# Expert weights in 2 MB loads and 16 KB slots, and the down bias inside one pair

## The chip, the core and the metric

The kernel runs on one core of a Trainium2 chip. The metric is the device time of one execution in microseconds (us). "MB" is 1024 KB where it counts a load, and a rate in GB/s is as the profile gives it.

## What is computed

A batch of one with 256 tokens, 16 meta tokens put ahead of them, width 1024, one layer, all in float32: a layer norm, a mixer with two branches (attention with forget gates, and an S5 state space scan), a residual norm, and a mixture of 32 experts of which each token uses four.

```python
h = layer_norm(concat(meta, x), ln_in_g, ln_in_b)                  # 272 x 1024
proj = h @ w_in                                                    # q, k, v, f, u, gates a and b
y_a = forgetting_attention(q, k, v, log_sigmoid(f + b_f))
y_b = gelu(s5_ssm(u, a_re, a_im, log_dt, b, c, d)); y_b = y_b * sigmoid(y_b @ w_glu + b_glu)
mix = (sigmoid(g_a) * (y_a @ w_up_a) + sigmoid(g_b) * (y_b @ w_up_b)) @ w_o
h = layer_norm(ALPHA * h + mix, ln1_g, ln1_b)
top_v, top_i = top_k(h @ w_router + b_router, 4); comb = softmax weights scattered to 32 columns
for e in range(32):
    gate = minimum(h @ w_gate[e] + b_gate[e], 7)
    up = clip(h @ w_up[e] + b_up[e], -7, 7)
    out += comb[:, e:e + 1] * (((up + 1) * gate * sigmoid(1.702 * gate)) @ w_down[e] + b_down[e])
return layer_norm(ALPHA * h + out, ln2_g, ln2_b)[:, 16:]
```

## The kernel before

**The front** (0 to about 283 us) is everything up to the router. Weights of the projections come in slabs (`slab`, L104) of 2 MB, each as two loads of 1 MB into two 8 KB slots of pool `wA`. `wA` has six slots, so three slabs stand at a time; the next waits until TensorE (PE) has used an old one. Small operands come between them: the router weights `wr` (L567) and its bias `brow` (L568) are loaded after the third slab that `w_in` gives behind the small loads. GpSimd (POOL) multiplies `wr` by the columns of the layer norm (`wrg`, L675 and L677), and VectorE (DVE) reduces that to `wsum` (L676, L678), which is used only much later, by the router. On the same two engines run the S5 preparation: sine and cosine by powers on DVE (`sn`, `cs`, `ew`), then `lr` (L358), the complex coefficients, the powers `E`, the matrices `bb`, and on POOL `cL`, `q` and `bz`. DVE then starts the forget gate (`fx`, `fa`, L535 and L536), ScalarE (ACT) finishes it (L537) and empties the projection tiles `kA`, `qA` from PSUM (L550 to L556), then `bT` (L462), which PE needs for the scan's `pb` (L481). PE runs the projections (`ps`, L214) and the transposes of `bz` (L461) between them. The order on each engine in the front is set by a scheduler, from the order of the code and its own estimates; each engine then runs its instructions strictly in that order.

**The experts** run in pairs, 15 pairs and then two single ones. PE and SP follow the order of the code here. Each expert has three matrices of 4 MB. `gate_up` (L1062) computes gate and up for 64 rows of gathered tokens, `act_T` transposes, `down` (L1094) does the down product of both experts of a pair, `combine` (L1124) adds the pair's result to `acc`. A matrix comes in quarters: 256 rows, two rows to a partition, 1 MB, with 8 KB in one piece per partition (`expert_load`, L728). Eight matmuls use one quarter in `gate_up`.

All of these loads are issued by SP on one queue, in the order in which PE uses them. Each waits for its slot to be free and for the load eight places before it, since completions go around eight counters (`DMAHW0` to `DMAHW7`). Slots are given in a fixed rota (`homes`): five of `wC`, seven of `wB`, six of `wA`, and the storage of `gate1` and `hT`, 20 slots, to which the storage of `acc` is added once, so 21 MB stand in SBUF before PE starts the experts. The last quarter of all is loaded as two halves (L711).

The rows of the down bias `b_down` (32 x 1024) are loaded in pair 5 into a slot of the rota (L717) and multiplied by the routing weights in pairs 8 and 9 (`down_bias`).

Of the kernel before, what the change touches and what calls it, by code (L numbers as in the profile page):

```python
# [20 lines left out]
P = 128  # L21
D = 1024
# [11 lines left out]
NWA, NWB, NWC = 6, 7, 5  # L34
# [14 lines left out]
def hybrid_trunk_kernel(ctx: ExitStack, tc: tile.TileContext, x, meta, ln_in_g, ln_in_b, w_in, b_f,  # L49
# [44 lines left out]
    prowP = sp.tile([8, 256], F32, name="prowP")  # L94
    ldt = sp.tile([16, 2], F32, name="ldt")

    def slab(src, kt):

        n = src.shape[1]
        src = src.rearrange("(k p) n -> p k n", p=P)  # L100
        nk, ks = 2048 // n, []
        for k0 in range(0, kt, nk):
            v_ = wA.tile([P, 2048], F32, name="w", tag="w").rearrange("p (k n) -> p k n", n=n)
            nc.sync.dma_start(v_, src[:, k0:k0 + nk])  # L104
            ks += [v_[:, k] for k in range(nk)]
        return ks
# [21 lines left out]
    for j, a in enumerate((ln1_g, ln1_b)):  # L128
        nc.sync.dma_start(prowP[4 * j:4 * j + 4], a.rearrange("l (q n) -> (l q) n", n=256))
# [140 lines left out]
    for k in range(2):  # L270
        TE.transpose(pp[:, 8 * k:8 * k + 8], prowP[:, k::2], ident[:8, :8])
# [438 lines left out]
    def part_load(t_, w, e, qtr, k):  # L710
        nc.sync.dma_start(t_[:, k], w[0, e, 256 * qtr:256 * qtr + 256].rearrange("(p k) n -> k p n", k=2)[k])  # L711

    def load_rows(rows):
        pool, tag = home[nload[0]]
        nload[0] += 1
        t_ = pools[pool].tile([P, 2048], F32, name="w", tag=tag)[:rows.shape[0], :D]
        nc.sync.dma_start(t_, rows)  # L717
        return t_

    def expert_load(w, e, qtr, load=True):  # L720
        key = (w.tensor.name, e, qtr)
# [37 lines left out]
    prefetch(2)  # L759
# [39 lines left out]
    prefetch(NWB - 4)  # L799
# [250 lines left out]
    def gate_up(e, between=None):  # L1050
        c0 = CAP * (e % 2)
        pos_ = []
        for j, (w, tag) in enumerate(((w_gate, "pg"), (w_up, "pu"))):
            pt = pg.tile([P, 512], F32, name=tag, tag=tag)
            for qtr in range(4):
                if between and (j, qtr) == (1, 1):
                    between()
                wt = expert_load(w, e, qtr)
                for k in range(2):
                    kk = 2 * qtr + k  # L1060
                    for n in range(2):
                        TE.matmul(pt[64 * n:64 * n + 64], XT[:, kk, c0:c0 + CAP], wt[:, k, n * 512:n * 512 + 512],  # L1062
# [24 lines left out]
    def down(p, aTs):  # L1087
        Yp = [py_.tile([P, 512], F32, name="Yp", tag=f"Yp{n}") for n in range(2)]
        for qtr in range(4):
            wd = [expert_load(w_down, 2 * p + g, qtr) for g in range(2)]  # L1090
            for k, n in ((0, 0), (0, 1), (1, 0), (1, 1)):
                half, j = qtr // 2, 2 * (qtr % 2) + k
                for g in range(2):
                    TE.matmul(Yp[n][64 * g:64 * g + 64], aTs[g][:, j, half],  # L1094
                              wd[g][:, k, n * 512:n * 512 + 512],
                              start=qtr == 0 and k == 0, stop=qtr == 3 and k == 1, skip_group_check=True)
# [3 lines left out]
    def down_one(e, aT):  # L1100

        Y = py_.tile([P, 512], F32, name="Yp", tag=f"Yp{e % 2}")
        for qtr in range(4):
            wd = expert_load(w_down, e, qtr)
            for k in range(2):
                half, j = qtr // 2, 2 * (qtr % 2) + k
# [248 lines left out]
```

## Time and profile before

| | us |
|---|---|
| median of 3 runs | 1225.4 |
| lowest, highest | 1223.43, 1225.46 |
| the profiled execution | 1222.52 |
| its span | 1221.0 |
| PE busy, share of the span | 1124.1, 92% |
| DVE busy, share | 340.4, 28% |
| ACT busy, share | 177.3, 15% |
| POOL busy, share | 71.6, 6% |
| chain that ended last | DMA 53%, PE 38%, DVE 5% |

The busy share of PE counts what it does at whatever pace the data allow. The chain that ended last is followed back from the last instruction, at each step to what released it. A stretch of it on DMA is time in which a load was under way on whose end the next step hung.

### The profile page before, as it was taken

How to read it: one execution, taken by the hardware profiler on the slowest of the kernel's cores; microseconds unless marked ns; L12 is line 12 of the kernel's file. 1: busy time of each engine (PE TensorE's matmuls, PEld its weight loads, DVE VectorE, ACT ScalarE, POOL GpSimd, SP SyncE). 2: the span in 40 equal slices, each digit the busy share in tenths (PEclk: the TensorE clock that was granted, in tenths of full speed). 3: DMA queues.
4: the chain of work that ended last, by engine and by line, in shares of the span. 5: the costliest groups of instructions: out<-in, count | busy, mean ns of one | idle time of the engine just before them, and what ended most of it. 6: DMA issues, size and time to landing. Idle time of an engine off the chain costs nothing.

```text
span 1221.0 us, 13200 instructions
## 1 busy us (share of the span) xinstructions
PE 1124.1 (92%) x5398; PEld 588.9 (48%) x5399; DVE 340.4 (28%) x782; ACT 177.3 (15%) x387; POOL 71.6 (6%) x118
## 2 busy tenths in 40 slices
PE   4889999998999999999999999998999899998994
PEld 2777788754545444444434363535433343443331
DVE  3969420533221212112131312130212121202013
ACT  2357410311101011010101010101010111101000
POOL 3333200400000000000000000000000000000001
PEclk9999999998999999999999999999999999999998
DMA  7742289557999999999999999999999999999992
GB/s 150 187 105 69 104 211 357 221 208 301 413 422 420 423 420 421 422 420 407 421 422 422 421 422 421 421 421 419 422 420 422 421 421 421 421 421 420 422 421 104
DMA packets 75674, 433.60 MB, mean 355 GB/s; under 512 B 14218, under 2 KB 14570, under 8 KB 26586
## 3 DMA queue, kind: packets, MB, share of 16 engines
q1 hardware_dynamic: 75178, 432.19, 89.3%
q8 instruction: 44, 0.72, 0.2%
q10 hardware_dynamic: 432, 0.52, 0.1%
q14 instruction: 20, 0.16, 0.0%
HBM read 431.64 MB, written 1.05 MB: 354 GB/s over the span
## 4 chain that ended last, share of the span: by engine, by line
DMA 53%; PE 38%; DVE 5%; ACT 1%; issue 1%; POOL 1%; SPq 1%; POOLq 0%; ACTq 0%; DVEq 0%
DMA w<-in_w_up_dram 29%; DMA w<-in_w_down_dram 16%; PE ps L214 7%; PE pu L1062 6%; PE pg L1062 6%; PE Yp L1094 5%; DMA w<-in_w_gate_dram 5%; PE ps L764 2%; PE px L945 2%; DMA w<-in_b_down_dram 2%; PE Yp L1108 1%; PE ps L936 1%; PE po L936 1%; PE px L1124 1%; DMA prow<-in_ssm_a_im_dram 1%
## 5 line engine op out<-in xcount | busy, mean ns | idle before, releaser
L1062 PE MATMUL pu<-w,xy 128*64 128x512 f32 x1024 | 238.5, 595 | 13.5 <-DMA w<-in_w_up_dram 13.5
L1062 PE MATMUL pg<-w,xy 128*64 128x512 f32 x1024 | 236.9, 594 | 3.3 <-PEq L1153 2.1
L1094 PE MATMUL Yp<-w,aT 128*64 128x512 f32 x960 | 228.1, 611 | 0.0
L1094 PEld LDWEIGHTS Yp<-w,aT 128*64 128x64 f32 x960 | 101.5, 141 | 114.7 <-issue 99.1
L1062 PEld LDWEIGHTS pu<-w,xy 128*64 128x64 f32 x1024 | 81.4, 136 | 154.8 <-issue 108.9
L1062 PEld LDWEIGHTS pg<-w,xy 128*64 128x64 f32 x1024 | 86.6, 137 | 140.4 <-issue 134.0
L214 PE MATMUL ps<-hT,w 128*128 128x256 f32 (+1 forms) x512 | 119.3, 392 | 2.8 <-ACT pr L595 2.8
L214 PEld LDWEIGHTS ps<-hT,w 128*128 128x128 f32 x512 | 98.0, 194 | 19.7 <-ACT pr L595 3.1
L1072 DVE TENSOR_SCALAR pg<-pg 128x512 f32<-128x512 f32 x32 | 22.4, 699 | 232.7 <-PE pg L1065 232.7
L1073 ACT ACTIVATE ups<-pg 128x512 f32<-128x512 f32 x32 | 19.1, 597 | 415.3 <-DVE pg L1072 415.3
L1075 DVE TENSOR_SCALAR pu<-pu 128x512 f32<-128x512 f32 x32 | 22.4, 700 | 186.8 <-PE pu L1065 186.8
L1097 DVE COPY xy<-Yp 128x512 f32<-128x512 f32 x15 | 10.4, 692 | 223.3 <-PE Yp L1094 223.3
L1124 PE MATMUL px<-xy,selT 128*128 128x512 f32 x120 | 61.7, 636 | 4.7 <-DVE acc L1126 2.6
L945 PE MATMUL px<-sel,z 128*128 128x128 f32 x480 | 59.8, 283 | 0.6 <-DVE sel L950 0.6
L1313 POOL TENSOR_TENSOR acc<-acc,gb 128x512 f32<-128x512 f32 (+1 forms) x2 | 2.4, 1214 | 979.6 <-ACT acc L1311 979.6
L945 PEld LDWEIGHTS px<-sel,z 128*128 128x128 f32 x480 | 58.6, 196 | 0.8 <-ACT aT L1084 0.8
L1124 PEld LDWEIGHTS px<-xy,selT 128*128 128x128 f32 x120 | 20.4, 193 | 42.3 <-DVE acc L1126 19.2
L1126 DVE TENSOR_TENSOR acc<-acc,px 128x512 f32<-128x512 f32 x56 | 37.3, 683 | 12.3 <-PE px L1124 12.2
L1098 ACT COPY xy<-Yp 128x512 f32<-128x512 f32 x15 | 8.8, 586 | 218.3 <-PE Yp L1094 218.3
L1084 ACT COPY aT<-px 128x512 f32<-128x512 f32 x32 | 18.8, 586 | 133.6 <-PE px L1082 133.6
L885 DVE TENSOR_SCALAR xy<-px,pcolP 128x128 f32<-128x128 f32 x60 | 23.7, 410 | 45.4 <-ACT xy L887 43.4
L887 ACT ACTIVATE xy<-px,pcolP 128x128 f32<-128x128 f32 x60 | 25.8, 455 | 44.6 <-PE px L945 42.6
(399 smaller groups left out, 838.2 us busy)
## 6 DMA issues: line engine op xcount, KB each, us to landing
w<-in_w_gate_dram SPq DMA_DIRECT2D x128, 1024.0 KB
w<-in_w_up_dram SPq DMA_DIRECT2D x128, 1024.0 KB
w<-in_w_down_dram SPq DMA_DIRECT2D x127, 1024.0 KB
w<-in_w_in_dram SPq DMA_DIRECT2D x16, 1024.0 KB
w<-in_w_o_dram SPq DMA_DIRECT2D x4, 1024.0 KB
w<-in_w_up_a_dram SPq DMA_DIRECT2D x2, 1024.0 KB
w<-in_w_up_b_dram SPq DMA_DIRECT2D x2, 1024.0 KB
w<-in_w_glu_dram SPq DMA_DIRECT2D x1, 1024.0 KB
```

Source lines behind the costliest of these rows:

```text
L214: TE.matmul(pt, w[k][:, j * P:(j + 1) * P], hT[:, k, n0:n1], start=k == 0, stop=k == KD - 1)
L764: TE.matmul(pt, w[k][:, d * P:(d + 1) * P], y[:, k], start=k == 0, stop=k == 3)
L885: V.tensor_scalar(out_, in_, g_, b_, op0=ALU.mult, op1=ALU.add)
L887: S.activation(out_, in_, AF.Identity, scale=g_, bias=b_)
L936: TE.matmul(po[i][n], mT[:, k, i * P:(i + 1) * P], wo[k // 2][:, k % 2, n * 512:n * 512 + 512], start=False, stop=k == KD - 1, skip_group_ ...
L945: TE.matmul(pts[k // 4][:, (k % 4) * P:(k % 4 + 1) * P], z1[:, i, paired(k)], sel[:, i].rearrange("p e s -> p (e s)"), start=i == 0 and k ...
L1062: TE.matmul(pt[64 * n:64 * n + 64], XT[:, kk, c0:c0 + CAP], wt[:, k, n * 512:n * 512 + 512], start=kk == 0, stop=False, skip_group_check=True)
L1072: V.tensor_scalar_min(pgt, pgt, 7.0)
L1075: V.tensor_scalar(put, put, 7.0, -7.0, op0=ALU.min, op1=ALU.max)
L1094: TE.matmul(Yp[n][64 * g:64 * g + 64], aTs[g][:, j, half], wd[g][:, k, n * 512:n * 512 + 512], start=qtr == 0 and k == 0, stop=qtr == 3 an ...
L1124: TE.matmul(pt, selT[:, i * P:(i + 1) * P], Ysb[:, ns], start=True, stop=True)
L1126: V.tensor_add(acc[:, i, ns], acc[:, i, ns], pt)
```

## The change

An expert's matrix comes in halves: 512 rows, four rows to a partition, 2 MB, with 16 KB in one piece per partition. The slots are 16 KB: four of `wA`, three of `wB`, two of `wC`. The storage of `gate1` and `hT` serves as one place of the rota together, as two loads of 1 MB; in the first round `acc` and `gate1` serve so. That makes ten places, 20 MB. The last half of all also comes as two loads of 1 MB. Which row of an expert's input stands on which partition (`paired`, the columns of the layer norm `pcolP`) follows the new layout. A slab of the front takes one `wA` slot of 16 KB, still with two loads of 1 MB, and four slabs stand at a time. `w_o` takes two slots instead of four. Load and use of `b_down` are both in pair 8. What the two kernels do when an expert has more than 64 tokens (`crowded`) is rewritten for the new slots too; with these inputs that branch isn't taken, and the diff leaves it out.

```diff
--- before
+++ after
-NWA, NWB, NWC = 6, 7, 5
+NWA, NWB, NWC = 4, 3, 2
...
-    prowP = sp.tile([8, 256], F32, name="prowP")
+    prowP = sp.tile([P, 512], F32, name="prowP", tag="etmp")[:4]
...
     def slab(src, kt):
 
         n = src.shape[1]
         src = src.rearrange("(k p) n -> p k n", p=P)
-        nk, ks = 2048 // n, []
+        nk = 2048 // n
+        v_ = wA.tile([P, 4096], F32, name="w", tag="w").rearrange("p (k n) -> p k n", n=n)
         for k0 in range(0, kt, nk):
-            v_ = wA.tile([P, 2048], F32, name="w", tag="w").rearrange("p (k n) -> p k n", n=n)
-            nc.sync.dma_start(v_, src[:, k0:k0 + nk])
-            ks += [v_[:, k] for k in range(nk)]
-        return ks
+            nc.sync.dma_start(v_[:, k0:k0 + nk], src[:, k0:k0 + nk])
+        return [v_[:, k] for k in range(kt)]
...
-    slots = [("wC", "w")] * NWC + [("wB", "w")] * (NWB - 4) + [("wA", "w")] * NWA + [("keep", "gate1")]
-    slots += [("wB", "w")] * 4 + [("fk", "hT")]
-    first = slots[:NWC + NWB + NWA - 3] + [("keep", "acc")] + slots[NWC + NWB + NWA - 3:]
+    PAIR = (("keep", "gate1"), ("fk", "hT"))
+    slots = [(("wC", "w"),)] * NWC + [(("wB", "w"),)] * (NWB - 2) + [(("wA", "w"),)] * NWA + [PAIR]
+    slots += [(("wB", "w"),)] * 2
+    first = slots[:NWC + NWB + NWA - 2] + [(("keep", "acc"), ("keep", "gate1"))] + slots[-2:]
...
-        while len(out) <= 12 * NE:
-            out += [s_ for s_ in slots if s_ != ("keep", "gate1") or len(out) < 9 * NE - 24]
-        return out[:12 * NE + 1]
+        while len(out) <= 6 * NE:
+            out += [s_ for s_ in slots if s_ != PAIR or len(out) < 9 * NE // 2 - 12]
+        return out[:6 * NE + 1]
...
-    def part_load(t_, w, e, qtr, k):
-        nc.sync.dma_start(t_[:, k], w[0, e, 256 * qtr:256 * qtr + 256].rearrange("(p k) n -> k p n", k=2)[k])
+    def part_load(t_, w, e, hf_, k0, nk):
+        nc.sync.dma_start(t_, w[0, e, 512 * hf_:512 * hf_ + 512].rearrange("(p k) n -> p k n", k=4)[:, k0:k0 + nk])
...
-    def expert_load(w, e, qtr, load=True):
-        key = (w.tensor.name, e, qtr)
+    def expert_load(w, e, hf_, nk=4):
+
+        key = (w.tensor.name, e, hf_)
         if key in ready:
             return ready.pop(key)
-        pool, tag = home[nload[0]]
+        place = home[nload[0]]
         nload[0] += 1
-        t_ = pools[pool].tile([P, 2048], F32, name="w", tag=tag).rearrange("p (k n) -> p k n", n=D)
-        if load:
-            nc.sync.dma_start(t_, w[0, e, qtr * 256:qtr * 256 + 256].rearrange("(p k) n -> p k n", k=2))
-        return t_
+        ks = []
+        for pool, tag in place:
+            n = 4 // len(place)
+            t_ = pools[pool].tile([P, n * D], F32, name="w", tag=tag).rearrange("p (k n) -> p k n", n=D)
+            for k0 in range(0, n, nk):
+                part_load(t_[:, k0:k0 + min(n, nk)], w, e, hf_, len(ks) + k0, min(n, nk))
+            ks += [t_[:, k] for k in range(n)]
+        return ks
...
     def paired(k):
 
-        return slice(256 * (k // 2) + k % 2, 256 * (k // 2) + 256, 2)
+        return slice(512 * (k // 4) + k % 4, 512 * (k // 4) + 512, 4)
...
-            for qtr in range(4):
+            for hf_ in range(2):
...
-                wt = expert_load(w, e, qtr)
-                for k in range(2):
-                    kk = 2 * qtr + k
+                wt = expert_load(w, e, hf_)
+                for k in range(4):
+                    kk = 4 * hf_ + k
...
         upA = activate(0, *gate_up(2 * p))
-        if p == 5:
+        if p in (6, 7):
+            residual(p - 6)
+        elif p == 8:
             bdown = [load_rows(b_down[0])]
-        elif p in (6, 7):
-            residual(p - 6)
-        elif p in (8, 9):
-            down_bias(p - 8)
+            for i in range(2):
+                down_bias(i)
...
-    for qtr in range(3):
-        ready[w_down.tensor.name, e + 1, qtr] = expert_load(w_down, e + 1, qtr)
-    last = expert_load(w_down, e + 1, 3, load=False)
-    for k in range(2):
-        part_load(last, w_down, e + 1, 3, k)
-    ready[w_down.tensor.name, e + 1, 3] = last
+    for hf_ in range(2):
+        ready[w_down.tensor.name, e + 1, hf_] = expert_load(w_down, e + 1, hf_, 4 - 2 * hf_)
```

On SP, in the front, from the first slab behind the small loads: before, `w_125` to `w_131` are two slabs, `w_613` and `w_615` the third.

```order
L104 DMA w_125<-in_w_in_dram 128x4x512 [waits DMAHW1_49]
L104 DMA w_127<-in_w_in_dram 128x4x512 [waits DMAHW2_49]
L104 DMA w_129<-in_w_in_dram 128x4x512 [waits DMAHW3_49]
L104 DMA w_131<-in_w_in_dram 128x4x512 [waits DMAHW4_49]
L104 DMA w_613<-in_w_in_dram 128x4x512 [waits DMAHW5_49,PE_49]
L104 DMA w_615<-in_w_in_dram 128x4x512 [waits DMAHW6_49,PE_49]
L567 DMA wr_133<-in_w_router_dram 128x8x32 [waits DMAHW7_49]
L568 DMA brow_134<-in_b_router_dram 1x32 [waits DMAHW0_49]
```

The same stretch of SP after the change:

```order
L104 DMA w_124<-in_w_in_dram 128x4x512 [waits DMAHW1_49]
L104 DMA w_124<-in_w_in_dram 128x4x512 [waits DMAHW2_49]
L104 DMA w_127<-in_w_in_dram 128x4x512 [waits DMAHW3_49]
L104 DMA w_127<-in_w_in_dram 128x4x512 [waits DMAHW4_49]
L104 DMA w_612<-in_w_in_dram 128x4x512 [waits DMAHW5_49]
L104 DMA w_612<-in_w_in_dram 128x4x512 [waits DMAHW6_49]
L566 DMA wr_130<-in_w_router_dram 128x8x32 [waits DMAHW7_49]
L567 DMA brow_131<-in_b_router_dram 1x32 [waits DMAHW0_49]
```

The third slab (`w_612`) keeps its place ahead of `wr`, and has lost its wait for PE.

On DVE, in the front, around `lr`, the first coefficient of the scan; before:

```order
L352 TENSOR_SCALAR ew<-ew 128x144 [waits DVE_49]
L350 SCALAR_TENSOR_TENSOR ew<-sn,cs 128x144 [waits DVE_49]
L358 TENSOR_TENSOR lr<-mag,ew 128x16 [waits DVE_49]
L361 TENSOR_TENSOR zi<-mag,ew 128x16 [waits DVE_49]
L424 COPY E_488<-ew 128x32
L359 TENSOR_SCALAR zr<-lr 128x16 [waits DVE_49]
L367 TENSOR_TENSOR t_419<-zi,pcol 128x16 [waits DVE_49]
```

and after:

```order
L351 TENSOR_SCALAR ew<-ew 128x144 [waits DVE_49]
L349 SCALAR_TENSOR_TENSOR ew<-sn,cs 128x144 [waits DVE_49]
L675 TENSOR_REDUCE wsum<-wrg 128x32 [waits Pool_49]
L357 TENSOR_TENSOR lr<-mag,ew 128x16 [waits DVE_49]
L360 TENSOR_TENSOR zi<-mag,ew 128x16 [waits DVE_49]
L423 COPY E_487<-ew 128x32
L678 TENSOR_TENSOR wsum<-wsum,brow 1x32 [waits DMAHW0_49,DVE_49]
L358 TENSOR_SCALAR zr<-lr 128x16 [waits DVE_49]
```

The reduction of `wrg` to `wsum`, which stood 57 places behind `lr` (row 173 of this engine), stands just ahead of it, and its second step, which needs `brow`, three places behind.

On POOL, the multiplication of `wr` that this reduction waits for; before, from the clearing of `vmz` to the first `wrg`:

```order
L623 MEMSET vmz 128x512 [waits DMAHW5_49,DMAHW4_49,DVE_49]
L406 TENSOR_TENSOR cL_478<-cT_458,lr 128x512 [waits DVE_49,Activation_49]
L406 TENSOR_TENSOR cL_479<-cT_459,lr 128x512 [waits Activation_49]
L407 TENSOR_TENSOR q_480<-cT_459,zi 128x512 [waits DVE_49,PE_49]
L407 TENSOR_TENSOR q_484<-cT_458,zi 128x512 [waits PE_49]
L408 TENSOR_TENSOR cL_478<-cL_478,q_480 128x512 [waits Pool_49]
L408 TENSOR_TENSOR cL_479<-cL_479,q_484 128x512 [waits Pool_49]
L449 TENSOR_SCALAR bz<-bb 64x4x16 [waits DVE_49]
L449 TENSOR_SCALAR bz<-bb 64x4x16 [waits Pool_49]
L449 TENSOR_SCALAR bz<-bb 64x4x16 [waits DVE_49]
L449 TENSOR_SCALAR bz<-bb 64x4x16
L675 TENSOR_TENSOR wrg<-wr,pcol 128x256 [waits DMAHW7_49,Pool_49]
```

and after:

```order
L622 MEMSET vmz 128x512 [waits DMAHW5_49,DMAHW4_49,DVE_49]
L674 TENSOR_TENSOR wrg<-wr,pcol 128x256 [waits DMAHW7_49]
L676 TENSOR_TENSOR wrg<-wr,pcol 128x256 [waits DVE_49]
L405 TENSOR_TENSOR cL_477<-cT_457,lr 128x512 [waits DVE_49,Activation_49]
L405 TENSOR_TENSOR cL_478<-cT_458,lr 128x512 [waits Activation_49]
L406 TENSOR_TENSOR q_479<-cT_458,zi 128x512 [waits DVE_49,PE_49]
L406 TENSOR_TENSOR q_483<-cT_457,zi 128x512 [waits PE_49]
```

Both multiplications of `wr` have moved ahead of the products with `cT`.

On SP, at the end of the program, from the gate load of expert 30 on; before:

```order
L728 DMA w<-in_w_gate_dram 128x2048 x4
L728 DMA w<-in_w_up_dram 128x2048 x4
L728 DMA w<-in_w_down_dram 128x2048 x4
L728 DMA w<-in_w_gate_dram 128x2048 x4
L728 DMA w<-in_w_up_dram 128x2048 x4
L728 DMA w<-in_w_down_dram 128x2048 x3
L711 DMA w<-in_w_down_dram 128x1024 x2
```

and after:

```order
L712 DMA w<-in_w_gate_dram 128x4096 x2
L712 DMA w<-in_w_up_dram 128x4096 x2
L712 DMA w<-in_w_down_dram 128x4096 x2
L712 DMA w<-in_w_gate_dram 128x4096 x2
L712 DMA w<-in_w_up_dram 128x4096 x2
L712 DMA w<-in_w_down_dram 128x4096
L712 DMA w<-in_w_down_dram 128x2048 x2
```

The order is the same, in half as many loads.

## Rows read from the trace of the kernel before

**Rows 1.** The page: GB/s in 40 slices of 30.5 us, and packets.
```profile
GB/s 150 187 105 69 104 211 357 221 208 301 413 422 420 423 420 421 422 420 407 421 422 422 421 422 421 421 421 419 422 420 422 421 421 421 421 421 420 422 421 104
DMA packets 75674, 433.60 MB, mean 355 GB/s; under 512 B 14218, under 2 KB 14570, under 8 KB 26586
```

**Rows 2.** The chain that ended last: start, us, engine, line, instructions.
```profile
440.17 19.79 DMA w<-in_w_down_dram
...
1139.34 20.03 DMA w<-in_w_up_dram
1159.42 1.94 PE pu L1062 x8
...
1216.94 0.82 POOLq L1351
```

**Rows 3.** Windows: stretch, us, busy PE, PEld, DVE, ACT, POOL (instructions), PEclk, DMA, GB/s.
```profile
340.00:550.00 210.00, 203.00 (x966) 93.71 (x964) 43.98 (x75) 19.61 (x39) 0.00 (x0) 1.00 1.01 421
850.00:1190.00 340.00, 317.96 (x1461) 132.40 (x1458) 62.16 (x104) 30.32 (x59) 0.00 (x0) 0.98 1.01 421
```

**Rows 4.** Timeline of PE: start, us, instruction, [idle before, and what ended it].
```profile
283.75 7.26 PE L1062 MATMUL pg<-w,xy 128*64 128x512 f32 x32 [0.50 <-ACT xy L887]
```

**Rows 5.** Windows around the start of the experts.
```profile
280.00:286.00 6.00, 5.50 (x28) 3.94 (x28) 1.93 (x7) 1.37 (x3) 0.00 (x0) 0.66 0.00 0
286.00:294.00 8.00, 8.00 (x40) 2.63 (x38) 1.81 (x4) 2.34 (x3) 0.00 (x0) 1.00 0.88 315
```

**Rows 6.** Timeline of SP's queue: issues in the front and at the first freed slots.
```profile
24.67 23.93 SPq L104 DMA_DIRECT2D w<-in_w_in_dram  x6
48.65 0.50 SPq L567 DMA_DIRECT2D wr<-in_w_router_dram  x1
...
285.90 3.76 SPq L728 DMA_DIRECT2D w<-in_w_down_dram  x3
```

**Rows 7.** Waits of SP's queue from 0 to 60 us: total, times, longest.
```profile
SPq L104 <- PE ps L214: 18.9, 2, 17.5
```

**Rows 8.** Windows in the front, around the third slab.
```profile
38.00:45.00 7.00, 6.63 (x27) 5.35 (x25) 7.00 (x32) 1.56 (x3) 2.44 (x3) 0.76 0.98 334
45.00:47.00 2.00, 2.00 (x10) 1.65 (x10) 2.00 (x5) 0.00 (x0) 2.00 (x3) 1.00 0.08 30
47.00:56.00 9.00, 9.00 (x41) 7.47 (x40) 8.97 (x31) 0.78 (x3) 3.54 (x5) 1.00 0.88 248
```

**Rows 9.** Timeline of DVE in the front.
```profile
42.77 0.16 DVE L358 TENSOR_TENSOR lr<-mag,ew 128x16 f32<-128x16 f32 x1
...
61.72 0.59 DVE L676 TENSOR_REDUCE wsum<-wrg 128x32 f32<-128x256 f32 x1 [0.51 <-POOL wrg L675]
```

**Rows 10.** Timeline of POOL in the front.
```profile
62.40 0.62 POOL L677 TENSOR_TENSOR wrg<-wr,pcol 128x256 f32<-128x256 f32 x1 [0.71 <-DVE wsum L676]
```

**Rows 11.** Timeline of ACT in the front.
```profile
60.57 0.43 ACT L537 ACTIVATE fa<-fa 128x272 f32<-128x272 f32 x1 [5.90 <-DVE fa L536]
...
69.02 0.38 ACT L551 COPY kA<-ps 64x272 f32<-64x272 f32 x1
...
74.27 0.59 ACT L462 COPY bT<-ps 128x512 f32<-128x512 f32 x1
```

**Rows 12.** Timeline of PE in the front, 15 to 235 us.
```profile
51.70 21.74 PE L214 MATMUL ps<-hT,w 128*128 128x272 f32 x96
73.27 0.60 PE L461 MATMUL ps<-ident,bz 128*128 128x128 f32 x4
...
74.91 1.19 PE L481 MATMUL pb<-ux,bT 128*128 128x136 f32 x8 [0.78 <-ACT bT L462]
227.28 8.04 PE L764 MATMUL ps<-ya__1272,w 128*128 128x256 f32 x36 [2.54 <-DVE ya__1272 L809]
```

**Rows 13.** Windows: `w_o` in pieces of 4 KB, and a burst of expert loads.
```profile
184.00:192.00 8.00, 8.00 (x39) 7.04 (x38) 0.84 (x2) 0.38 (x1) 0.00 (x0) 1.00 1.03 417
244.00:250.00 6.00, 6.00 (x15) 2.66 (x14) 0.00 (x0) 0.00 (x0) 0.00 (x0) 1.00 1.01 426
```

More of the change, by code (lines that the diff above doesn't have):

```diff
@@ L783, in hybrid_trunk_kernel @@
     wo = []
-    for i in range(4):
-        t_ = wB.tile([P, 2048], F32, name="w", tag="w").rearrange("p (k n) -> p k n", n=D)
-        nc.sync.dma_start(t_, w_o[0, 256 * i:256 * i + 256].rearrange("(k p) n -> p k n", p=P))
+    for i in range(2):
+        t_ = wB.tile([P, 4096], F32, name="w", tag="w").rearrange("p (k n) -> p k n", n=D)
+        for h_ in range(2):
+            nc.sync.dma_start(t_[:, 2 * h_:2 * h_ + 2],
+                              w_o[0, 512 * i + 256 * h_:512 * i + 256 * h_ + 256].rearrange("(k p) n -> p k n", p=P))
         wo.append(t_)
@@ L1088, in down @@
         Yp = [py_.tile([P, 512], F32, name="Yp", tag=f"Yp{n}") for n in range(2)]
[L1089 to L1096, printed above, removed]
+        for hf_ in range(2):
+            wd = [expert_load(w_down, 2 * p + g, hf_) for g in range(2)]
+            for k in range(4):
+                for n in range(2):
+                    for g in range(2):
+                        TE.matmul(Yp[n][64 * g:64 * g + 64], aTs[g][:, k, hf_],
+                                  wd[g][k][:, n * 512:n * 512 + 512],
+                                  start=hf_ == 0 and k == 0, stop=hf_ == 1 and k == 3, skip_group_check=True)
         V.tensor_copy(Ysb[:, :512], Yp[0])
@@ L1102, in down_one @@
         Y = py_.tile([P, 512], F32, name="Yp", tag=f"Yp{e % 2}")
[L1103 to L1106, printed above, removed]
+        for hf_ in range(2):
+            wd = expert_load(w_down, e, hf_)
+            for k in range(4):
                 for n in range(2):
-                    TE.matmul(Y[64 * n:64 * n + 64], aT[:, j, half], wd[:, k, n * 512:n * 512 + 512],
-                              start=qtr == 0 and k == 0, stop=qtr == 3 and k == 1, skip_group_check=True)
+                    TE.matmul(Y[64 * n:64 * n + 64], aT[:, k, hf_], wd[k][:, n * 512:n * 512 + 512],
+                              start=hf_ == 0 and k == 0, stop=hf_ == 1 and k == 3, skip_group_check=True)
         return Y
@@ L1154, in crowded @@
             free = list(slots)
-            for s_ in home[nload[0] - 8:nload[0]]:
+            for s_ in home[nload[0] - 4:nload[0]]:
                 free.remove(s_)
-            free = [s_ for s_ in free if s_[0] != "keep"]
-            free.sort(key=lambda s_: ("wC", "fk", "wB", "wA").index(s_[0]))
+            free = [s_[0] for s_ in free if s_ != PAIR]
             def slot(n):
                 pool, tag = free[n]
-                return pools[pool].tile([P, 2048], F32, name="w", tag=tag)
-            h1Td = slot(0).rearrange("p (k t) -> p k t", k=KD)
+                return pools[pool].tile([P, 4096], F32, name="w", tag=tag)
+            both = slot(0)
+            h1Td = both[:, :2048].rearrange("p (k t) -> p k t", k=KD)
             for k in range(KD):
@@ L1184, in crowded @@
                     nc.gpsimd.dma_start(bu, b_up[0, bass.ds(e, 1), :])
-                    aT = slot(2).rearrange("p (k t) -> p k t", k=KD)
-                    wg_e, wu_e = weights_of(w_gate, 3), weights_of(w_up, 7)
+                    if len(free) > 5:
+                        aT = slot(5)[:, :2048]
+                    else:
+                        aT = fk.tile([P, 2048], F32, name="w", tag="hT")
+                    aT = aT.rearrange("p (k t) -> p k t", k=KD)
+                    tg_, tu_ = ([slot(n + hf_).rearrange("p (k n) -> p k n", n=D) for hf_ in range(2)] for n in (1, 3))
+                    wg_e, wu_e = weights_of(w_gate, tg_), weights_of(w_up, tu_)
                     for i in range(2):
@@ L1223, in hybrid_trunk_kernel @@
             for w in (w_gate, w_up):
-                for qtr in range(4):
-                    ready[w.tensor.name, 2 * p, qtr] = expert_load(w, 2 * p, qtr)
+                for hf_ in range(2):
+                    ready[w.tensor.name, 2 * p, hf_] = expert_load(w, 2 * p, hf_)
             order.close()
```

56 lines of the change are left out of this document (28 added, 28 removed).

## The prediction

> **What bounds the kernel now.** I read the page first, for the rate of the loads over time, then the chain of waits, then windows of the stretches that it names, and last the timelines of the engines in the front. In the 40 slices the rate climbs to about 421 GB/s behind slice 10 and stays there until the last slice [rows 1]. The chain is TensorE (PE) up to 440 us; from there to 1159.42 us it consists for the most part of links on loads of the expert weights, of about 19.8 us each [rows 2]. A load waits for the one eight places before it, so a link of 19.8 us is eight loads of 2.48 us: the queue works them off one behind the other. From 1159.42 us on the chain is work again, 1216.94 + 0.82 at its end. The windows say the same in a rate: 421 GB/s with the DMA share at 1.01 in the middle and late stretch, while PE is busy too [rows 3]. 1 MB (1.0486 million bytes) at 421 GB/s takes 2.491 us.
>
> So the time is a sum of three. First, the front until PE starts the experts at 283.75 us [rows 4]. Until then every slot is full and nothing moves: 0 GB/s in 280 to 286 [rows 5]; the first load follows the first freed slot, at 285.90 [rows 6]. Then comes the stream up to the last up load of expert 30 (368 MB of which 21 stand ready, so 347), and then a tail of PE work of some 61 us behind it. A change counts if it moves the start of the stream, its bytes, its rate or the tail. PE's busy share of 92% doesn't set the end in the stream, but in the front PE is the engine that is waited for.
>
> **The front: +10.0 us.** Before, the third slab finds no free slot: SP waits 18.9 us for PE [rows 7], and only then issues the third slab's loads and, at 48.65, `wr` [rows 6]. The queue stands nearly still in 45 to 47 [rows 8]. With a fourth slot that wait goes. What comes instead is in the order: DVE reduces `wrg` ahead of `lr`, and POOL makes `wrg` ahead of `cL`, so both now wait for `wr` to land, and `wr` stands in the queue behind six loads of 1 MB. In the trace DVE is at `lr` at 42.77 [rows 9]. When does `wr` land? The first four loads and the small ones are through when the queue runs empty at about 45 [rows 8]. What is left is 2 MB; at the 334 GB/s of the window before, 6.3 us, at 421 GB/s, 5.0 us: `wr` lands at 50 to 51.5, with a us or two until its end is seen 51 to 53.5. I take 52.6. POOL's product is 0.62 us [rows 10], the reduction 0.59 [rows 9]: `lr` comes at 53.8 instead of 42.77, **+11.0 us**, and the wait for SP that went is worth nothing, since PE's weights were there in time.
>
> Who is late with it? All that DVE does from `lr` to the forget gate shifts by 11: `fa` is done for ACT at about 71.6 instead of 60.57. ACT empties `kA` and `qA` from PSUM behind `fa`, in fixed order; the first key tile but one leaves at 69.40 [rows 11], so at 80 to 82 in the changed kernel. PE has six PSUM buffers for these tiles: it has run its 96 matmuls from 51.70 without a wait [rows 12], and now stands until a buffer comes free, so the transposes of `bz`, at 73.27, come at 81 to 82, `bT`, at 74.27 on ACT, at about 85, and `pb`, at 74.91, at 85.7: +10.8 us. From there to 283.75 PE has little idle time to catch up in. One wait of 2.54 us, at 227.28 [rows 12], may shrink; I count 0.8 of it. **+10.0**, with 5 (`wr` 3 us earlier, the whole of that wait back) and 14 (`wr` 3 us later, as behind the bias row too) as ends.
>
> **The start of the stream: +1.8 and +2.5.** A slot of 2 MB is free after 16 matmuls of `gate_up`, one of 1 MB after eight. 32 take 7.26 us [rows 4], so eight more are 1.8 us, in which the queue stands idle. And 20 MB stand ready instead of 21: 1 MB more must come through the stream, 2.5 us. Both end at the start of the stream, with nothing beside them.
>
> **The tail: +1.8.** Behind the last up load of expert 30 PE has eight matmuls to do, 1.94 us [rows 2]; it now has 16. The last two loads stay 1 MB, and come in time as before: what PE needs of them comes 40 us after 1159.42.
>
> **The rate: -8 us.** This is the term that the trace doesn't show, since no load in it has pieces of 16 KB. 348 MB fall into the stream; 14 of the 192 halves (those in the storage of `gate1`, `hT` and `acc`, and the last) still come as two loads, so 93%, 324 MB, change. Two rows are near. `w_o`, in pieces of 4 KB, came at 417 GB/s [rows 13], 2.515 us per MB; pieces of 8 KB at 2.491. If a fixed cost per piece makes the difference of 0.024, the next doubling gives half, 0.012 x 324 = 3.9 us. A burst of 6 us of 8 KB pieces came at 426 GB/s [rows 13], 2.461 us per MB: if larger pieces and half as many loads gave that for good, 9.7 us. Ends: as far above 426 as it lies above 421, 431 GB/s or 2.433 us, -18.8; and on the other side a loss as large as the step from 8 KB down to 4 KB, 0.024 x 324 = +7.8. I take **-8**, nearer to the burst, because half the loads go too, which the step between the pieces leaves out.
>
> The Trainium skill, on the page DMA: Bandwidth & Descriptors, section "Where 436 GB/s comes from", puts the ceiling of the ports at 435.2 GB/s and says that loads from HBM are held at about 358 GB/s. The row of 421 disagrees with the second; by the first the term could be no better than -26, an estimate. The same page, section "Rules for kernel authors", asks for at least 1 MiB per DMA for the full bandwidth; loads of 1 MB have that already, so by this rule the rate would not move, and the sum would be that of rival B below.
>
> **No cost.** The bias rows in pair 8: the rows are one small load with the pair's weights, behind the loads of expert 16; PE finds eight or more matmuls and the combine to do while it lands, and it is issued once in either kernel. If that cover failed, PE would wait about 2 us, inside a stretch where the loads set the pace. Four transposes for `prowP` instead of two, the other strides of `paired`, and `w_o` in two slots keep the number of bytes and, but for two small transposes, of PE instructions. SP has half as many loads to issue; it isn't late before.
>
> **Sum.** 10.0 + 1.8 + 2.5 + 1.8 - 8 = +8.1 us. The profiled execution took 1222.52 (span 1221.0), so 1230.6; the median of the runs, 1225.4, is 2.9 above it: **1233.5 us**.
>
> **Rivals.** Two per mille of the time, 2.5 us, is about what this measurement can tell from no change: same is 1222.9 to 1227.9.
>
> A: the front is not later. `wr` is small, and if it lands by 41.5 us (42.77 less POOL's and DVE's two steps), or if PE has enough other work while DVE waits, the +10.0 is gone: 6.1 - 8 = -1.9, **1223.5**. For it: SP issues `wr` some 15 us earlier than before, and the queue no longer stands still. Against: the links of 19.8 us show a queue that works loads off in order [rows 2], and 6 MB stand ahead of `wr`.
>
> B: the rate does not move; pieces of 8 KB have reached what the queue gives, or the pieces of 16 KB are cut up on their way. Then +16.1, **1241.5**. For it: 417 to 421 is a small step for twice the piece, and the DMA share is full at either [rows 3, 13]. Against: the 426 of the burst.
>
> C, which ends on the other side: the larger pieces bring the rate to 431 GB/s. Then 16.1 - 18.8 = -2.7, **1222.7**. It outweighs the other terms from 2.441 us per MB on, 429.5 GB/s. For it: half as many loads and pieces, and a burst already 5 GB/s above the mean. Against: no stretch of the trace reaches it. A and C together give -12.7, 1212.7.
>
> **Chances.** Forecast 0.42 (own range 1227 to 1240, from the front's and the rate's ends), A 0.18, B 0.18, C 0.16, A and C together 0.06. A and C lie at the edge between faster and same, so about half of each falls on either side: faster 0.08 + 0.09 + 0.06 = 0.23; same 0.10 + 0.07 and 0.03 from the forecast's low end = 0.20; slower the rest of the forecast and B, 0.39 + 0.18 = 0.57. From 1219 to 1243 leaves out A with C, and the far ends of B and of the front.
>
> **What would show it.** In the changed kernel: DVE idle from about 42.8 to 53 before the reduction of `wrg`, ended by POOL, and POOL by `wr`; `pb` at about 86 and the first `gate_up` at about 294; the first freed slot 3.6 us behind that; a window of the middle at 424 to 427 GB/s. Packets of 8 KB and more, 49,088 before [rows 1], fall to about 26,400 if the pieces of 16 KB stay whole. The prediction is wrong if `lr` runs at 43 us (A), if the middle stands at 421 (B) or at 430 and above (C), or if the queue has gaps in the stream because slots of 2 MB come free too late.

## The result and the profile after

The changed kernel takes **1278.0 us** (median of 4 runs, 1275.57 to 1282.58) against 1224.4 of the kernel before on the same chip: a ratio of 1.044, 95% interval 1.0417 to 1.0464, or 53.6 us slower. The profiled execution took 1282.58 us, span 1281.0. The forecast was 1233.5, and its range ended at 1243: the sign was right, the size was not, and the largest price stood in no term of the sum.

The page after; the lines that answer to [rows 1], with the shares of the chain:

```profile
GB/s 150 236 67 1 118 215 381 173 173 295 343 429 405 426 421 428 409 430 420 427 415 425 382 366 399 426 336 348 273 428 426 429 426 427 428 426 428 429 340 33
DMA packets 50031, 433.57 MB, mean 338 GB/s; under 512 B 11366, under 2 KB 11710, under 8 KB 23474
...
PE 26%; DVE 2%; ACT 1%; POOL 0%; issue 0%; POOLq 0%; ACTq 0%
```

Packets of 8 KB and more are 50,031 - 23,474 = 26,557, where 26,400 were forecast: the pieces of 16 KB stay whole. In slices of 32 us the rate reaches 426 to 430 GB/s, more than before, but in six slices between 700 and 930 us it falls to between 273 and 399. And in the chain, which is followed back to 906.96 us here, there is no DMA left. One pair of it, late in the stream, where before links of 19.8 us on loads stood [rows 2] (start, us, what):

```profile
1108.11 7.02 PE pg L1070 x32
1115.12 0.22 PE pg L1073 x2
1115.34 6.87 PE pu L1070 x32
1122.21 0.22 PE pu L1073 x2
1122.43 0.68 PE px L1090 x4
1123.11 7.46 PE px L953 x32
...
1133.68 15.26 PE Yp L1102 x64
```

TensorE (PE) sets the pace now. In the kernel before it waited 13.5 us for up loads; in the changed kernel it waits for no load in the stream. The groups of the up product on both pages, before and then after (the last column is the idle time ahead of them and what ended it):

```profile
L1062 PE MATMUL pu<-w,xy 128*64 128x512 f32 x1024 | 238.5, 595 | 13.5 <-DMA w<-in_w_up_dram 13.5
```
```profile
L1070 PE MATMUL pu<-w,xy 128*64 128x512 f32 x1024 | 232.6, 592 | 0.0
```

The odd line of the chain is L953, the gather of the next pair's tokens: 32 matmuls of 128 x 128 in 7.46 us. The groups on the page of before (L945), busy us and mean ns, matmuls and weight loads:

```profile
L945 PE MATMUL px<-sel,z 128*128 128x128 f32 x480 | 59.8, 283 | 0.6 <-DVE sel L950 0.6
L945 PEld LDWEIGHTS px<-sel,z 128*128 128x128 f32 x480 | 58.6, 196 | 0.8 <-ACT aT L1084 0.8
```

and of after:

```profile
L953 PE MATMUL px<-sel,z 128*128 128x128 f32 x480 | 114.3, 397 | 0.6 <-DVE sel L958 0.6
L953 PEld LDWEIGHTS px<-sel,z 128*128 128x128 f32 x480 | 113.1, 329 | 0.8 <-ACT aT L1092 0.8
```

Same count, same shape, 54.5 us more of PE's time in the whole. What changed is the layout of the weight operand: `z1[:, i, paired(k)]` takes every fourth float of a row (a step of 16 bytes) where it took every second (8 bytes).

The front went nearly as forecast. The timelines of SP, POOL, DVE and PE after, which answer to [rows 6, 9, 10, 12]:

```profile
39.81 2.29 SPq L566 DMA_DIRECT2D wr<-in_w_router_dram  x1
```
```profile
54.13 0.61 POOL L674 TENSOR_TENSOR wrg<-wr,pcol 128x256 f32<-128x256 f32 x1 [14.09 <-DMA wr<-in_w_router_dram]
```
```profile
54.78 0.60 DVE L675 TENSOR_REDUCE wsum<-wrg 128x32 f32<-128x256 f32 x1 [11.14 <-POOL wrg L674]
55.29 0.17 DVE L357 TENSOR_TENSOR lr<-mag,ew 128x16 f32<-128x16 f32 x1
```
```profile
75.61 0.63 PE L460 MATMUL ps<-ident,bz 128*128 128x128 f32 x4
81.84 0.43 PE L465 MATMUL ps<-cT,bz 128*32 128x32 f32 x8 [5.60 <-ACT kA L550]
85.59 2.18 PE L480 MATMUL pb<-ux,bT 128*128 128x136 f32 x8 [3.32 <-ACT bT L461]
...
296.87 7.09 PE L1070 MATMUL pg<-w,xy 128*64 128x512 f32 x32 [0.51 <-ACT xy L895]
```

SP issues `wr` 8.8 us earlier than before. DVE stands 11.14 us for POOL, POOL 14.09 us for the load of `wr`. `pb` starts at 85.59 (85.7 forecast), the experts at 296.87, 13.1 us later than in [rows 4].

### The profile page after: what moved, and what is told of

Same layout as the page of the kernel before. It is cut to its first block, busy times and chain, and to the rows that moved or that the text cites. A ratio compares the mean times of both kernels' runs of the same rounds, so it can differ in the third digit from the quotient of the medians.

```text
span 1281.0 us, 12903 instructions
## 1 busy us (share of the span) xinstructions
PE 1194.1 (93%) x5400; PEld 642.7 (50%) x5401; DVE 336.5 (26%) x782; ACT 177.3 (14%) x387; POOL 71.6 (6%) x118
## 2 busy tenths in 40 slices
DMA packets 50031, 433.57 MB, mean 338 GB/s; under 512 B 11366, under 2 KB 11710, under 8 KB 23474
## 3 DMA queue, kind: packets, MB, share of 16 engines
HBM read 431.64 MB, written 1.05 MB: 338 GB/s over the span
## 5 line engine op out<-in xcount | busy, mean ns | idle before, releaser
L1102 PE MATMUL Yp<-w,aT 128*64 128x512 f32 x960 | 236.5, 634 | 0.0
L1070 PE MATMUL pg<-w,xy 128*64 128x512 f32 x1024 | 233.0, 594 | 1.0 <-ACT xy L895 0.5
L1070 PE MATMUL pu<-w,xy 128*64 128x512 f32 x1024 | 232.6, 592 | 0.0
L1102 PEld LDWEIGHTS Yp<-w,aT 128*64 128x64 f32 x960 | 93.9, 147 | 133.2 <-issue 122.9
L1070 PEld LDWEIGHTS pg<-w,xy 128*64 128x64 f32 x1024 | 82.3, 137 | 141.1 <-issue 138.5
L1070 PEld LDWEIGHTS pu<-w,xy 128*64 128x64 f32 x1024 | 84.7, 137 | 130.8 <-issue 126.6
L213 PE MATMUL ps<-hT,w 128*128 128x256 f32 (+1 forms) x512 | 122.0, 397 | 2.6 <-ACT pr L594 1.6
L953 PE MATMUL px<-sel,z 128*128 128x128 f32 x480 | 114.3, 397 | 0.6 <-DVE sel L958 0.6
L953 PEld LDWEIGHTS px<-sel,z 128*128 128x128 f32 x480 | 113.1, 329 | 0.8 <-ACT aT L1092 0.8
L1133 DVE TENSOR_TENSOR acc<-acc,px 128x512 f32<-128x512 f32 x56 | 37.3, 684 | 13.4 <-PE px L1131 13.4
```

The lines of the kernel that those rows point to most:

```text
L213: TE.matmul(pt, w[k][:, j * P:(j + 1) * P], hT[:, k, n0:n1], start=k == 0, stop=k == KD - 1)
L953: TE.matmul(pts[k // 4][:, (k % 4) * P:(k % 4 + 1) * P], z1[:, i, paired(k)], sel[:, i].rearrange("p e s -> p (e s)"), start=i == 0 and k ...
L1102: TE.matmul(Yp[n][64 * g:64 * g + 64], aTs[g][:, k, hf_], wd[g][k][:, n * 512:n * 512 + 512], start=hf_ == 0 and k == 0, stop=hf_ == 1 and ...
L1133: V.tensor_add(acc[:, i, ns], acc[:, i, ns], pt)
```

## The experiments

**1. Steps of the weight operand, by pair.** In the changed kernel each pair's gather takes another step:

```diff
-            TE.matmul(pts[k // 4][...], z1[:, i, paired(k)],
+            TE.matmul(pts[k // 4][...], z1[:, i, (k % 2) * min(st, 4):(k % 2) * min(st, 4) + 127 * st + 1:st],
...
+                gather_mm(pts, sel, i, (1, 2, 3, 4, 6, 7)[p % 6])
```

> The changed kernel, but pairs 1 to 15 gather with columns of z in steps of 1, 2, 3, 4, 6 or 7 elements (4 to 28 bytes) in turn, so the experts get other inputs than in the reference. Theory 1 (the step of the weight operand is what costs): a weight load of the gather takes 196 ns at steps of 1 and 2, 329 ns at 4 and above, and between them at 3. Rival (the 16 KB loads or the clock disturb TensorE, whatever the step): about 329 ns in every pair.

Measured: 1253.9 us, one run. The timeline of weight loads for pairs 1 to 6, with steps of 2, 3, 4, 6, 7 and 1 floats (start, us for all 32):

```profile
328.57 3.88 PEld L953 LDWEIGHTS px<-sel,z 128*128 128x128 f32 x32 [0.82 <-ACT aT L1092]
384.45 5.68 PEld L953 LDWEIGHTS px<-sel,z 128*128 128x128 f32 x32
442.33 7.54 PEld L953 LDWEIGHTS px<-sel,z 128*128 128x128 f32 x32
501.41 7.22 PEld L953 LDWEIGHTS px<-sel,z 128*128 128x128 f32 x32
561.50 7.49 PEld L953 LDWEIGHTS px<-sel,z 128*128 128x128 f32 x32
620.70 3.77 PEld L953 LDWEIGHTS px<-sel,z 128*128 128x128 f32 x32
```

Steps of one and two floats cost the same, three cost 1.5 times that, four twice, and beyond four it doesn't get worse. That is the shape of a price per 16 bytes touched: 128 floats touch 64 such lines at a step of two, 96 at three, 128 at four and more; below 64 (step one: 32) nothing more is won. Later pairs repeat it (5.68 at 736.53, 7.54 at 803.12), and the rival, a disturbance whatever the step, is out. The Trainium skill names a mechanism of this shape, on the page SBUF — State Buffer, section "Door 1: The DMA port swizzle": SBUF answers in lines of 16 bytes, and at least two accesses must hit a line to be served at full rate. The six rows agree. The same note goes on to allow a stride of four fp32 elements for free; here a step of four costs twice, and the measurement decides.

**2. The old step in the changed kernel.**

```diff
-            TE.matmul(pts[k // 4][...], z1[:, i, paired(k)],
+            TE.matmul(pts[k // 4][...], z1[:, i, 256 * (k // 2) + k % 2:256 * (k // 2) + 256:2],
```

> The changed kernel with one edit: the gather reads z in steps of two elements, as before, so the experts get their inputs in another order than in the reference. Theory 1: the 480 gather matmuls fall back from 397 to about 283 ns each, the pairs wait for the loads again, and the time is that of the front (+13.1), of the start of the stream and the tail (+1.8, +2.5, +1.8) and of a rate of 427 GB/s (-11.4): about 1230 to 1234. Rival 2 (slots of 2 MB come free too late and starve the queue): the time stays near 1278.

Measured: **1227.9 us** (1226.81 to 1229.28, 10 runs), ratio 1.0028 (1.0018 to 1.0038), somewhat below the 1230 to 1234 expected: the 13.1 us put in for the front held some 3 us that belong to the step (see experiment 4). The gather is back at 283 ns, and a window of the middle of the stream shows the loads as the bound, without gaps (columns as in [rows 3]):

```profile
340.00:550.00 210.00, 202.98 (x967) 95.20 (x964) 44.68 (x76) 19.62 (x39) 0.00 (x0) 1.00 1.01 426
```

One index of one operand carries 50 of the 53.6 us. Slots of 2 MB don't starve the queue: the gaps in the rate, which the prediction named as a sign of slots that come free too late, came from PE's pace.

**3. Loads of 2 MB in pieces of 8 KB.**

```diff
-        nc.sync.dma_start(t_, w[0, e, 512 * hf_:512 * hf_ + 512].rearrange("(p k) n -> p k n", k=4)[:, k0:k0 + nk])
+        r0 = 512 * hf_ + P * k0
+        nc.sync.dma_start(t_.rearrange("p (b k) n -> p b (k n)", k=2),
+                          w[0, e, r0:r0 + P * nk].rearrange("(b p k) n -> p b (k n)", p=P, k=2))
```

> The changed kernel with slots and loads of 2 MB, each in two pieces of 8 KB per partition, so that the rows and the step of two elements are as before; it computes the reference. Theory 1: the gather costs what it cost before. If the better rate comes from half as many loads, it stays at 427 GB/s and the time is about 1231; if it comes from the larger piece, it falls to 421 GB/s and the time is about 1242. Rival 2 (slots too coarse): near 1278 at either.

Measured: **1242.8 us** (1241.03 to 1244.11, 4 runs), ratio 1.0143 (1.0117 to 1.0169). Its late stretch:

```profile
860.00:1040.00 180.00, 164.87 (x780) 72.11 (x778) 33.48 (x57) 17.47 (x34) 0.00 (x0) 0.99 1.01 421
```

421 GB/s, the rate of [rows 3], with loads twice as large. So the better rate, 426 to 427, comes from the piece of 16 KB and not from the number of loads.

**4. The reduction of the router's weights held back.**

```diff
+    with tc.issue_after(famark.ins), tc.issue_after(clmark.ins):
+        G.tensor_mul(wrg, wr, bc(col(R_L1B, KD), 2, NE))
+        V.tensor_reduce(wsum[:, 1], wrg.rearrange("p k n -> p n k"), AX.X, ALU.add)
```

(`famark` is the instruction of `fa`, `clmark` the last of `cL`.)

> The changed kernel with one edit: the reduction of the router weights and its product are held behind the forget gate on VectorE and behind cL on GpSimd, as in the order before. The front's theory: lr runs at 43 us again, the first gate_up at about 284 instead of 296.9, and since TensorE sets the pace behind it, the whole 12 to 13 us are gained: about 1266. Rival (the front is late for another reason, such as the loads of the slabs): first gate_up at 295, time 1278.

Measured: **1265.8 us** (1263.80 to 1276.65, 4 runs), ratio 1.0353 (1.0296 to 1.0410). DVE and PE:

```profile
44.60 0.16 DVE L357 TENSOR_TENSOR lr<-mag,ew 128x16 f32<-128x16 f32 x1
```
```profile
76.94 1.19 PE L480 MATMUL pb<-ux,bT 128*128 128x136 f32 x8 [0.78 <-ACT bT L461]
...
286.96 8.83 PE L1071 MATMUL pg<-w,xy 128*64 128x512 f32 x32 [0.49 <-ACT xy L896]
```

The stall in the front is worth 1278.0 - 1265.8 = 12.2 us, and its cause is the place of two instructions. The size is loose, since the interval of this run is about 7 us wide on either side; the same edit on top of experiments 3 and 5 gives 1242.8 - 1229.4 = 13.4 and 1228.5 - 1217.9 = 10.6. The experts start at 286.96 and not at 284: of the 13.1 us that they came late, 9.9 go with the reduction. Most of the other 3.2 is the first pair's gather, which stands in the front and has the slow step too: experiment 8, whose front is otherwise that of before, starts the experts at 286.26, 2.5 us late.

**5. z stored in the order in which the gather reads it.** ScalarE's copies of z out of PSUM write it in the experts' order, the router's weights are loaded in that order too, and the residual reads z back in its own:

```diff
-                S.copy(z1[:, i, n * 512:n * 512 + 512], po[i][n])
+                S.copy(z1[:, i, n * 512:n * 512 + 512].rearrange("q (k p) -> q p k", k=4),
+                       po[i][n].rearrange("q (p k) -> q p k", k=4))
...
-            TE.matmul(pts[k // 4][...], z1[:, i, paired(k)],
+            TE.matmul(pts[k // 4][...], z1[:, i, k * P:(k + 1) * P],
```

> The changed kernel, computing the reference, with z stored in the order in which the gather reads it (ScalarE's copies out of PSUM write it so, and the router's weights stand in the same order), so that the gather's weight operand lies in one piece. Line theory: the gather's 32 weight loads of a pair take 3.8 us instead of 7.5, the pairs wait for the loads again, 1227 to 1230. Rival (the price is only moved, to the writes of z or to the router): the start of the experts is 3 us or more later than 296.9, time 1231 or more.

Measured: **1228.5 us** (1227.06 to 1229.07, 4 runs), ratio 1.0041 (1.0027 to 1.0056). Here the experts get the inputs that they should, at the time of experiment 2. The copies of z take 1.04 to 1.05 us instead of 0.59; the experts start at 295.14, not later.

**6. Both repairs.**

> Both repairs in the changed kernel: z in order, and the reduction of the router weights held behind the forget gate. If the two prices are separate and the loads set the pace: 1228 less 10 or 11, 1217 to 1219, below the kernel before. If the front's delay is partly given back in the stream anyway: 1222 or more.

Measured: **1217.9 us** (1215.49 to 1221.05, 6 runs), ratio **0.9955** (0.9941 to 0.9969): a little faster than the kernel before, with the whole interval below 1. In a second set of runs, whose expectation was

> The kernel with both repairs once more, on the same chip as the kernel with the bias spread: 1216 to 1219, 0.994 to 0.997 of the kernel before.

it took 1217.4 us (1216.38 to 1220.90, 7 runs), ratio 0.9934 (0.9909 to 0.9959). Windows of the first:

```profile
340.00:550.00 210.00, 202.99 (x968) 93.67 (x966) 43.82 (x75) 19.59 (x39) 0.00 (x0) 1.00 1.01 427
860.00:1040.00 180.00, 167.15 (x795) 76.78 (x791) 33.35 (x57) 17.47 (x34) 0.00 (x0) 0.99 1.01 427
```

**7. Slots of 2 MB alone**: experiment 3 with the reduction held back.

> Slots and loads of 2 MB in pieces of 8 KB, and the reduction held back: what is left against the kernel before is the size of the slots alone. By the sum (start of the stream 1.8 and 2.5, tail 1.8, front 3.2 as the first gate_up of the run with the reduction held back showed): 1233. If the slot size is free: 1227.

Measured: **1229.4 us** (1228.83 to 1230.19, 4 runs), ratio 1.0049 (1.0034 to 1.0064). The experts start at 284.08, 0.3 us behind [rows 4], not 3.2 us: without that the expectation was 1230. So the slots cost 5.5 us, where 1.8 + 2.5 + 1.8 = 6.1 was the sum, and the pieces of 16 KB give back 1229.4 - 1217.9 = 11.5 (with the reduction not held back, experiments 3 and 5, 1242.8 - 1228.5 = 14.3).

**8. The step of four in the kernel before.** The edit of experiment 2 turned around, in the kernel before:

```diff
-            TE.matmul(pts[k // 4][...], z1[:, i, paired(k)],
+            TE.matmul(pts[k // 4][...], z1[:, i, 512 * (k // 4) + k % 4:512 * (k // 4) + 512:4],
```

> The kernel before with one edit: the gather reads z in steps of four elements, so the experts get their inputs in another order than in the reference. TensorE's pair then takes 54.5 + 3.7 = 58.2 us or a little more. If TensorE's time from its start at 284 decides (15 pairs, then the gate and up of expert 30): the last up ends at about 1172 to 1180 instead of 1161, time 1237 to 1244. If the loads still set the pace, since a pair's loads take 59.9 us: 1224 to 1226.

Measured: **1265.9 us** (1262.62 to 1267.27, 4 runs), ratio 1.0338 (1.0323 to 1.0353): 42 us, with nothing else of the change. That PE would become the bound was right, the size missed by more than 20 us. Windows from the first `gate_up` to the last up product of expert 30, before and then with the step of four (columns as in [rows 3]), tell why:

```profile
283.75:1161.36 877.61, 831.55 (x3896) 376.22 (x3896) 178.53 (x308) 81.95 (x161) 0.00 (x0) 0.99 1.01 418
```
```profile
286.26:1203.89 917.63, 888.05 (x3896) 422.13 (x3896) 179.15 (x308) 81.87 (x161) 0.00 (x0) 0.97 0.98 402
```

PE is busy for 56.5 us more, 54.5 of it in the gather. Against that stood only the time in which it had waited for loads, 13.5 us for up and 0.8 for gate weights in the whole stream, 14.3; that is gone. 54.5 - 14.3 = 40.2, and the stream is 40.0 us longer; the late start adds 2.5. The expectation had taken PE's plain pair for all fifteen.

The time from one pair's gather to the next shows the early part, in which no load is waited for (us between the starts of the gather's weight loads, worked out from the timelines; pairs 1 to 5):

```
before              54.4 54.5 54.5 54.5 54.5
after with wsum held back  59.0 58.1 58.1 58.1 58.1
before, step four   60.3 59.2 60.3 59.2 60.3
changed kernel      59.3 60.5 59.2 60.3 59.2
```

54.5 + 3.6 = 58.1 is the price of the weight loads alone. The other 0.9 to 2.4 us go with the clock. Windows of the changed kernel behind one gather (the eighth column is the granted clock):

```profile
508.00:512.00 4.00, 4.00 (x19) 4.00 (x19) 0.00 (x0) 0.09 (x1) 0.00 (x0) 1.00 1.02 430
512.00:516.00 4.00, 2.59 (x12) 2.10 (x12) 2.19 (x6) 1.82 (x5) 0.00 (x0) 0.80 1.02 434
516.00:520.00 4.00, 4.00 (x11) 1.59 (x11) 0.24 (x1) 0.77 (x2) 0.00 (x0) 0.50 0.98 418
```

and of the kernel before, in the same place of a pair:

```profile
475.00:479.00 4.00, 4.00 (x29) 2.52 (x25) 1.39 (x2) 0.59 (x1) 0.00 (x0) 1.00 1.01 422
479.00:483.00 4.00, 2.59 (x22) 2.40 (x22) 1.59 (x5) 1.72 (x4) 0.00 (x0) 1.00 1.01 418
483.00:487.00 4.00, 3.85 (x18) 1.84 (x20) 0.77 (x2) 0.96 (x2) 0.00 (x0) 1.00 1.02 422
```

Behind the slow gather, in which PE passes 19 matmuls in 4 us and then waits for 1.4 us, the clock stands at 0.50, the 1.2 GHz level, for about 4 us, and the first matmuls of the down product run at half speed. Behind the quick gather of this window it stays at full speed. Neither is a rule. Counted in windows of 2 us, the clock falls behind 13 of the 15 gathers of the stream in the changed kernel, 10 in this experiment, 1 in experiment 6, and 5 in the kernel before, all of these from 703 us on, such as

```profile
830.00:832.00 2.00, 2.00 (x6) 0.98 (x6) 0.00 (x0) 0.42 (x1) 0.00 (x0) 0.57 1.00 418
```

behind the gather at 822.91. Why it falls at one and not at the next was not tried. So the clock costs pairs 1 to 5 some 9 us here, but over the whole stream, where it falls before as well, PE's busy time grew by no more than 2.0 us beyond the gather's.

**9. The bias part undone**, on top of both repairs:

```diff
-        if p in (6, 7):
-            residual(p - 6)
-        elif p == 8:
-            bdown = [load_rows(b_down[0])]
-            for i in range(2):
-                down_bias(i)
+        if p == 5:
+            bdown = [load_rows(b_down[0])]
+        elif p in (6, 7):
+            residual(p - 6)
+        elif p in (8, 9):
+            down_bias(p - 8)
```

> The kernel with both repairs and the third part of the change undone: the rows of the down bias loaded in pair 5 and used in pairs 8 and 9, so that they hold a slot of 2 MB for four pairs. If the part costs nothing either way, as forecast: the same time as with both repairs, 1217 to 1219. If the held slot starves the queue: 2 us or more later, and the middle below 427 GB/s. If the crowded pair 8, which took 65.1 us, costs: earlier by 1 to 3 us.

Measured: **1238.5 us** (1233.48 to 1242.61, 6 runs), ratio 1.0103 (1.0071 to 1.0135): 21 us behind experiment 6 on the same chip. A window while the slot is held, and the same in experiment 6's second set:

```profile
660.00:680.00 20.00, 16.39 (x64) 6.25 (x62) 0.69 (x1) 0.58 (x1) 0.00 (x0) 0.83 0.70 280
```
```profile
660.00:680.00 20.00, 20.00 (x98) 9.27 (x96) 2.08 (x3) 1.18 (x2) 0.00 (x0) 1.00 1.01 425
```

The queue runs dry: the DMA share falls to 0.70 and PE's busy time from 20.00 to 16.39. The waits of SP for the last product with the bias rows, here and in experiment 6 (total, times, longest), show that a load stood for the slot:

```profile
SPq L715 <- PE px L1150: 26.0, 1, 26.0
```
```profile
SPq L715 <- PE px L1150: 0.2, 1, 0.2
```

In 620 to 680 SP stands 12.6 us for PE's down product. The cause as I read it: 128 KB of bias rows in a slot of 2 MB, held from pair 5 to pair 9, take one of ten places out of the rota; later loads wait for slots that PE frees later, and SP issues in order. Before, the same rows took one of 20 places for as long.

## Why the prediction was wrong

**Right: the front.** +10.0 was forecast; holding the reduction back gave 12.2, 13.4 and 10.6 us in three pairs of runs, and moved the start of the experts by 9.9. The chain from `wr` over `fa`, `kA`, a PSUM buffer and `bT` to `pb` was the one described. That `pb` came within 0.1 us is luck, though: `lr` came 1.5 us later than forecast (POOL started at 54.13, since `wr` landed later), and the way from `lr` to `pb` was 1.6 us shorter. The transposes of `bz`, forecast for 81 to 82, ran at 75.61; the product behind them (L465) stood, for 5.60 us. And `wr` was issued 8.8 us earlier than before, not some 15.

**Right: the slots.** 6.1 us forecast, 5.5 measured. **Nearly right: the rate**, -8 forecast, -11.5 to -14.3 measured. But the reason given for going beyond the half step (half as many loads) is wrong: 2 MB in pieces of 8 KB come at 421 GB/s. (The page of after counts 30 loads of 1 MB, so 15 halves came as two loads, where the prediction has 14; that moves nothing.)

**Wrong: "the other strides of `paired` ... keep the number of bytes and, but for two small transposes, of PE instructions", costed at nothing.** The count was right and the duration was not: 480 weight loads went from 196 to 329 ns. The diff shows the step go from two floats to four, and nothing in the sum asked who reads in that step. In the changed kernel this one edit is 1265.8 - 1217.9 = 47.9 us; experiments 2 and 5 give 50.1 and 49.5, and in the kernel before it is 42. Most of it is the weight loads themselves: PE's busy time in the stream differs by 65.9 us between experiments 4 and 6, 56.6 of it in the gather; the other 9.3 is what is left for the clock.

**Wrong: "PE's busy share of 92% doesn't set the end in the stream".** Taken alone it held for the kernel before. But it hid how little cover there was. A pair's loads take 59.9 us and a plain pair 54.5 us of PE time, which looks like 5.4 us per pair; but the pairs that carry the residual and the bias need more (58.6, 58.4 and 65.1 us for pairs 6 to 8 of experiment 6). Over the whole stream of 877.6 us PE waited for loads for 14.3 us, and that was all the cover for a step that costs 54.5. So experiment 8 shows 42 us at once where the loads' pace alone would show none. What I took as a stage with one bound had two, less than two per cent apart.

The four parts add up to 12.2 (front) + 47.9 (step of the gather) + 5.5 (slots) - 11.5 (pieces) = 54.1, with 53.6 measured. That proves nothing: each of the runs between the changed kernel and the kernel before stands in two of the differences, so they cancel whatever the parts are, and what is left is the difference between two medians of the kernel before, 1224.4 and 1223.8. What speaks for the parts is that those for the front, the step and the pieces were each measured in more than one pair of runs; that for the slots was measured once. The rivals were about the terms that were sized well (A, the front; B and C, the rate); none was about the operand.

That the bias part costs nothing inside the change was not shown. Where PE sets the pace it seems to cost a little: pairs 8 and 9 take 68.2 + 60.3 = 128.5 us in the changed kernel, with both steps of the bias in pair 8, and 62.5 + 62.2 = 124.7 us in experiment 8, with one in each. The old place, with slots this coarse, costs 21 us (experiment 9).

## What to carry to other kernels

When a layout changes, ask of every reader of it in what steps it reads: the weight operand of the gather could take every second float without a price, not every fourth. Before costing an edit at nothing because another engine sets the pace, add up how long the engine that you load waits for that one over the whole loop, not in a plain unit of it: here 14.3 us, for an edit of 54.5. And a change with one bad part can hide a good one: each part, taken alone, told more than the whole.

## What the hardware showed that was not expected

- The gather's weight loads of 128 x 128 floats are paid by lines of 16 bytes: 32 of them take 3.77 us at a step of one float, 3.88 at two, 5.68 at three, 7.54 at four.
- The transposes of `ups`, which also read in steps of two floats before and four after, don't suffer at the same clock. By the order of the names (in `pg<-w,xy` the second, `xy`, is loaded as weights) `ups` is a weight operand too, so the step alone doesn't make the price. What spares the transposes was not tried. A group of four on PE's timeline, before and then after:

```profile
1121.54 0.74 PE L1082 MATMUL px<-ident,ups 128*128 128x128 f32 x4
```
```profile
1122.36 0.75 PE L1090 MATMUL px<-ident,ups 128*128 128x128 f32 x4
```

- The size of the piece sets the rate in the long run: 421 GB/s at 8 KB whether the load has 1 or 2 MB, 427 at 16 KB. (For 4 KB there are only 8 us, at 417 GB/s [rows 13]; a burst of 6 us in pieces of 8 KB had 426.)
- The granted clock can fall to 0.50 behind a gather in which PE is shown as busy throughout (4.00 of 4.00 us) with 19 matmuls and as many weight loads, and a wait of 1.4 us; behind the quick gather, with 29 matmuls and the same wait, it fell less often (5 times of 15 against 13).
